# Attention by pairs of heads on half-array products, and a retention result laid out by features

## The chip, the cores and the metric

The kernel runs on one core of a Trainium2 chip. The metric is the device time of one execution in microseconds (us), as a median of several runs; lower is better. A core has a matrix engine (PE; the loading of its stationary operand is listed apart as PEld), a vector engine (DVE), a scalar engine (ACT), a general engine (POOL) and a queue that issues most of the transfers (SP). Each engine takes its instructions strictly in the order of its queue.

## The reference, cut to what matters

Two layers on 512 tokens of 1024 features. In each layer a modulated RMSNorm is projected to a wide vector, four mixers of 256 features each work on parts of it, one output projection and a SwiGLU follow. The change touches two mixers:

```python
def fox_attention(q, k, v, f_logit, f_bias):          # 4 heads of 64
    log_f = jax.nn.log_sigmoid((f_logit + f_bias).astype(jnp.float32))
    cum = jnp.cumsum(log_f, axis=1).transpose(0, 2, 1)
...
        s = jnp.einsum('bqhd,bkhd->bhqk', qb, k).astype(jnp.float32) * scale
        s = s + cq[..., :, None] - cum[:, :, None, :]
...
        p = jax.nn.softmax(s, axis=-1).astype(v.dtype)
        return jnp.einsum('bhqk,bkhd->bqhd', p, v)

def retention(q, k, v, g, positions, gn_g):            # 4 heads of 64, chunks of 128
...
    intra = jnp.einsum('bnhqk,bnkhe->bnqhe', intra_s, vc)
    kv = jnp.einsum('bnkhd,hk,bnkhe->bnhde', kc, zeta, vc)
...
        cross = jnp.einsum('bqhd,bhde->bqhe', q_n, state)
...
    o = (intra + cross).reshape(B, S, H, Dh).astype(jnp.float32)
    mu = jnp.mean(o, axis=-1, keepdims=True)
    var = jnp.mean(jnp.square(o - mu), axis=-1, keepdims=True)
    o = (o - mu) * lax.rsqrt(var + EPS) * gn_g.reshape(H, Dh).astype(jnp.float32)
    return jax.nn.silu(g) * o
```

## The kernel before, in words

Activations lie with features on the 128 partitions and the 512 tokens along the free axis. Every large projection is made of three products on split operands (`mm3`, lines 260 to 262), whose weights arrive by DMA in `raw` (L154, L152), are rounded on ACT (`wh`, L159) and corrected on DVE (`wl`, L164). Products of plain f32 operands, which the mixers use, appear in the trace as two passes each.

A layer runs the projections one after the other in the order of a written list (`MO` for layer 0, `MO1` for layer 1). The mixers are Python generators: `slot()`, called after each projection, advances every running generator by its rate from the table `KN`, so that their instructions are emitted between the projections. `finish_bg` runs a generator to its end where its result is needed. A scheduler then settles the order of each engine's queue. The output projection takes eight mixed pieces `mix[0..7]`: 0 and 1 from attention, 2 and 3 from pooling, 4 and 5 from retention, 6 and 7 from the convolution. Its first half (`do_o`) uses 2, 3, 6 and 7, the second half 0, 1, 4 and 5.

Attention (`fox_gen`) goes by single heads. `decay(h)` spreads the cumulated log forget gate of a head over all partitions with a product (L793), copies it (L795) and adds the causal mask (L797). `scores(h, i)` multiplies query block i with the keys up to it (L804; 64 rows of the array, since a head has 64 features), adds the decay while it takes the row minimum (L807, L811, L814), exponentiates on ACT (L816) and takes the reciprocal of the row sum (L817). `turn` transposes the unnormalized weights (L825) and copies them (L827), three steps later. `weigh` multiplies them with the values, four steps later (L838; 64 columns move), so that tokens come out on the partitions, and scales by the reciprocal (L841 on DVE in layer 0, L843 on ACT in layer 1). Once a pair of heads is done, four transposes (L847) bring features back to the partitions.

Retention (`ret_gen`) goes by pairs: transposed keys (L888), scores of both heads (L899), states (L913 to L921; here the two heads already write to the two column halves), results with tokens on the partitions (L931 on 128 rows, alternating with L933 on 64 rows), squares and their sums (L936, L938), normalization (L942), a transpose back (L949) and the product with the gate (L950). Rotary positions are applied on DVE (L875 to L879) from a copy that a DMA shuffles (L874).

The convolution (`conv_gen`) is 60 DVE instructions per layer (L735), then a normalization that goes PE, DVE, ACT, DVE, PE, DVE, POOL, PE (L741 to L753).

PSUM tiles come from two rings: three banks `mm` for projections, four banks `sm` for everything else.

Of the kernel before, what the change touches and what calls it, by code (L numbers as in the profile page):

```python
# [9 lines left out]
F32 = mybir.dt.float32  # L10
# [23 lines left out]
KN = {'GA': 3, 'GA1': 3, 'TR': 'V', 'NH': 5, 'NH1': 5, 'ST': ((0, 1), (1, 1), (2, 2), (4, 1), (5, 1), (6, 1), (7, 1)), 'bot': 1, 'MO': 'pu rk rq rg rv o o o o', 'MO1': 'pu rk rv rq o o o rg o', 'GK': 4, 'RD': 'sync', 'MM': 3, 'SM': 4, 'FB': 1, 'FB1': 2, 'FS': 'V', 'FS1': 'A', 'PT': 'A', 'PT1': 'A', 'LAGT': 3, 'LAGW': 4, 'OUTP': 0.0, 'FRONT': 1, 'FRONT1': 0, 'r_rot': 2, 'r_ada': 0.6, 'r_conv': 0.7, 'r_fox': 0.85, 'r_ret': 1, 'r_pool': 0.3, 'r_adaV': 0.4, 'q_conv': 1, 'q_fox': 1.2, 'q_ret': 2, 'q_pool': 0.4, 'q_adaV': 1, 'bP': 4, 'bPT': 2, 'bt': 3, 'brx': 2, 'bmx': 6, 'br8': 4, 'bpl': 3, 'brP': 3, 'bada': 3, 'bacs': 3, 'NR': 2, 'NW': 4, 'N1': 3, 'N11': 1, 'YLG': 9, 'SC': ('AVPPPGPA', 'GGPAVVPP', 'VVVVVVPP', 'VVVVVGVP', 'AAVPAVVP', 'VVVVVVVP', 'VVVVVVVP', 'AAVPAVVP'), 'SH': ('AVAPPPPP', 'VPPPPPAP', 'AAGAAAPP', 'AAAAAAPP', 'AAAAAAGP', 'AVVGAAVG', 'AAAAAAPP', 'AAAAAAPP'), 'MS': '', 'OF': {'lc': -1.907, 'lwq': -2.817, 'lw': -2.364, 'lh': -2.036, 'sc': -1.65, 'ds': 0.034, 'sh': -2.846, 'pc': -0.763, 'mc': -2.466, 'ph': -0.991, 'mh': 0.907, 't': 0.871, 'yh': -1.858, 'yl': 0.927, 'wh': -0.208, 'wl': -2.386, 'whq': -1.469, 'wlq': -0.219, 'mm': 0.333, 'mq': -0.566, 'dq': 0.84}, 'KB': (-4.084, -0.552, 1.672, 3.163, 4.202, 4.915, 6.134, 7.492), 'OA': (1, 0, 2, 3), 'OA1': (0, 1, 3, 2), 'OB': (1, 2, 0, 3), 'OB1': (1, 3, 0, 2), 'LAGW1': 4, 'LAGT1': 3, 'OUTP1': 3.0}  # L34
# [3 lines left out]
BUFS = dict(pw=2, ada=KN["bada"], ared=2, qk=4, acs=KN["bacs"], v=2, ff1=1, ff2=1, ff3=1, ff4=1, cumD=1, P=KN["bP"], rP=KN["brP"], PT=KN["bPT"], mx=KN["bmx"], ot=KN["bot"],  # L38
# [7 lines left out]
def trunk(ctx, tc, x, c, positions, ada_w, ada_b, norm_mix_g, norm_ffn_g, w_in, fox_fb,  # L46
# [8 lines left out]
    ps = ctx.enter_context(tc.tile_pool(name="ps", bufs=1, space=PSUM))  # L55

# [44 lines left out]
    sel = const([P, 32], "sel")  # L101
    eps = const([P, 1], "eps")
# [673 lines left out]
    def fox_gen(l, q, k, v):  # L776
# [10 lines left out]
        A.copy(cum[0:4, :], pt[0:4, :])  # L787
        yield
        head, prob, prT, outp, outt = {}, {}, {}, {}, {}

        def decay(h):
            pb = small()
            PE.matmul(pb, ident[0:4, h:h + 1].to_broadcast([4, P]), cum[0:4, :], start=True, stop=True)  # L793
            cb = held("ah1")
            A.copy(cb, pb)  # L795
            cd = tmp("cumD")
            V.tensor_tensor(out=tri(cd, P), in0=tri(cb, P), in1=tri(bigm, P).to_broadcast([P, 4, P]), op=ALU.add)  # L797
            head[h] = (cb, cd)

        def scores(h, i):  # L800
            cb, cd = head[h]
            pair, r0, w = h // 2, 64 * (h % 2), (i + 1) * P
            st = small()
            PE.matmul(st[:, 0:w], q[pair][r0:r0 + 64, i * P:w], k[pair][r0:r0 + 64, 0:w], start=True, stop=True)  # L804
            pr = tmp("P")
            mx = tmp("mx")
            V.tensor_tensor_reduce(out=pr[:, i * P:w], in0=st[:, i * P:w], in1=cd[:, i * P:w], scale=1.0,  # L807
                                   scalar=3e38, op0=ALU.add, op1=ALU.min, accum_out=mx[:, 0:1])
            m = mx[:, 0:1]
            if i > 0:  # L810
                V.tensor_tensor_reduce(out=pr[:, 0:i * P], in0=st[:, 0:i * P], in1=cb[:, 0:i * P], scale=1.0,  # L811
                                       scalar=3e38, op0=ALU.add, op1=ALU.min, accum_out=mx[:, 1:2])
                m = mx[:, 2:3]
                V.scalar_tensor_tensor(out=m, in0=mx[:, 0:1], scalar=mx[:, 1:2], in1=mx[:, 0:1],  # L814
                                       op0=ALU.min, op1=ALU.min)
            A.activation(pr[:, 0:w], pr[:, 0:w], AF.Exp, bias=m, scale=-1.0, accum_out=mx[:, 4:5])  # L816
            V.reciprocal(mx[:, 5:6], mx[:, 4:5])  # L817
            prob[h, i] = (pr, mx)

        def turn(h, i):  # L820
            pr, mx = prob.pop((h, i))
            w = (i + 1) * P
            tt = small()
            for j in range(i + 1):
                PE.transpose(tt[:, j * P:(j + 1) * P], pr[:, j * P:(j + 1) * P], ident)  # L825
            prT[h, i] = (tmp("PT"), mx)
            (A.copy if KL("PT", l) == "A" else V.tensor_copy)(prT[h, i][0][:, 0:w], tt[:, 0:w])  # L827

        def weigh(h, i):
            pair = h // 2  # L830
            pT, mx = prT.pop((h, i))
            if i == 0:
                outp[h] = small()
                if h % 2 == 0:
                    outt[pair] = tmp("ot")
            po = outp[h][:, i * 64:(i + 1) * 64]
            for j in range(i + 1):
                PE.matmul(po, pT[:, j * P:(j + 1) * P], v[:, j, h * 64:(h + 1) * 64], start=j == 0, stop=j == i)  # L838
            o = outt[pair][:, i * P + 64 * (h % 2):i * P + 64 * (h % 2) + 64]
            if KL("FS", l) == "V":  # L840
                V.tensor_scalar(out=o, in0=po, scalar1=mx[:, 5:6], scalar2=None, op0=ALU.mult)  # L841
            else:
                A.activation(o, po, AF.Copy, scale=mx[:, 5:6])  # L843
            if h % 2 == 1 and i == 3:
                pt = small()
                for t in range(4):
                    PE.transpose(pt[:, t * P:(t + 1) * P], outt[pair][:, t * P:(t + 1) * P], ident)  # L847
                mix[pair] = act_pair(pair)
                split(mix[pair], pt)

        todo = [(h, i) for h in range(4) for i in range(4)]
        decay(0)
        yield
        n = len(todo)
        for s_ in range(n + KL("LAGW", l)):
            if s_ < n:
                scores(*todo[s_])
            if 0 <= s_ - KL("LAGT", l) < n:
                turn(*todo[s_ - KL("LAGT", l)])
            if 0 <= s_ - KL("LAGW", l) < n:  # L860
                weigh(*todo[s_ - KL("LAGW", l)])
            if s_ < n and todo[s_][1] == 3 and s_ + 1 < n:
                decay(todo[s_][0] + 1)
            yield
# [16 lines left out]
    def ret_gen(l, pair, q, k, vbox, outs, sg):  # L881
# [433 lines left out]
```

## Time and profile before

| | |
|---|---|
| median of 3 runs (lowest, highest) | 1289.13 us (1285.33, 1296.54) |
| the profiled execution, its own time | 1290.33 us |
| its span, first to last instruction | 1288.5 us |
| mean granted PE clock | 0.964 |
| busy: PE, DVE, ACT, POOL | 1239.6, 758.0, 418.1, 100.8 us |
| attention's products on PE, layer 0 and layer 1 | 124 to 246 us, 755 to 825 us |
| retention's products on PE, layer 0 and layer 1 | 161 to 265 us, 818 to 864 us |
| convolution on DVE (L735), layer 0 and layer 1 | 80 to 186 us, 700 to 762 us |

The profile's page gives busy times, the groups of instructions and the waits. A busy time of PE counts overlapped and waiting matmuls in full, so the true step of a matmul is read from the chain of waits, which lists in order of time what ended last, with the count of instructions (x) in each piece.

### The profile page before, as it was taken

Reading aid. Unit: us, or ns where it says so; the run is one execution under the profiler, and the core shown is the slowest. Engines: PE = TensorE matmul, PEld = TensorE weight load, DVE = VectorE, ACT = ScalarE, POOL = GpSimd, SP = SyncE. Lnnn points to the kernel's source line nnn. Section 1 sums busy time; section 2 is a strip of 40 time slices with the busy share of each in tenths; the row PEclk is TensorE's granted clock in tenths of the full one; section 3 lists DMA queues with packets and bytes.
Section 4 is the critical chain, followed back from the end, with each engine's and each line's share of the span. In section 5 each row is a group of like instructions: output and inputs, shape, how many; then the busy total and the mean of one; then the engine's idle time right before and its main releaser. Section 6 shows DMA issues by size and latency. Waiting matters only on the chain.

```text
span 1288.5 us, 16684 instructions
## 1 busy us (share of the span) xinstructions
PE 1239.6 (96%) x6325; PEld 1029.5 (80%) x6325; DVE 758.0 (59%) x1324; ACT 418.1 (32%) x682; POOL 100.8 (8%) x183
## 2 busy tenths in 40 slices
PE   9999999999987999999999999889999999999997
PEld 8788677889875888888899877668988888888887
DVE  6789996467777655353357995355773333343333
ACT  5443333234221222222234244423432222222222
POOL 5542300101000000000000000000100000000000
PEclk8999977899998999999999999889999999999999
DMA  9766512124776736343233322012372333333321
GB/s 308 204 198 197 172 60 74 44 72 140 229 230 220 219 109 194 106 139 95 74 94 97 101 83 64 19 49 82 108 215 88 96 98 98 86 94 98 94 86 66
DMA packets 222552, 157.93 MB, mean 123 GB/s; under 512 B 8238, under 2 KB 197896, under 8 KB 222472
## 3 DMA queue, kind: packets, MB, share of 16 engines
q1 hardware_dynamic: 222312, 156.80, 40.7%
q8 instruction: 50, 0.82, 0.3%
q14 instruction: 30, 0.25, 0.1%
q10 hardware_dynamic: 160, 0.06, 0.0%
HBM read 152.64 MB, written 2.10 MB: 120 GB/s over the span
## 4 chain that ended last, share of the span: by engine, by line
PE 75%; DVE 5%; DMA 4%; issue 1%; ACT 1%; POOL 0%; DVEq 0%; SPq 0%; POOLq 0%; ACTq 0%
PE mm L260 22%; PE mm L261 21%; PE mm L262 21%; DMA ada<-in_ada_w 4%; PE sm L804 1%; DVE acs L315 1%; PE sm L838 1%; PE sm L931 1%; DVE wl L164 1%; PE sm L825 1%; PE sm L260 1%; PE sm L261 1%; PE sm L933 1%; PE sm L262 1%; PE sm L899 1%
## 5 line engine op out<-in xcount | busy, mean ns | idle before, releaser
L159 ACT CAST wh<-raw 128x1024 fp32r<-128x1024 f32 (+3 forms) x196 | 198.8, 1015 | 581.9 <-PE mm L261 354.9
L260 PE MATMUL mm<-yh,wh 128*128 128x512 f32 (+1 forms) x984 | 368.1, 381 | 7.3 <-ACT yh L433 6.5
L261 PE MATMUL mm<-yl,wh 128*128 128x512 f32 (+1 forms) x984 | 370.6, 378 | 2.8 <-DVE yl L437 2.8
L262 PE MATMUL mm<-yh,wl 128*128 128x512 f32 (+1 forms) x984 | 369.2, 377 | 0.0
L164 DVE TENSOR_TENSOR wl<-raw,wh 128x1024 fp32r<-128x1024 f32 (+3 forms) x196 | 231.5, 1181 | 137.1 <-ACT wh L159 131.5
L260 PEld LDWEIGHTS mm<-yh,wh 128*128 128x128 f32 x984 | 183.6, 189 | 43.5 <-ACT yh L433 7.6
L261 PEld LDWEIGHTS mm<-yl,wh 128*128 128x128 f32 x984 | 186.1, 189 | 39.2 <-DVE yl L437 3.8
L262 PEld LDWEIGHTS mm<-yh,wl 128*128 128x128 f32 x984 | 186.2, 189 | 36.1 <-issue 0.2
L260 PE MATMUL mm<-ah,wh 128*128 128x512 f32 (+1 forms) x516 | 191.3, 374 | 11.4 <-ACT ah L474 8.8
L261 PE MATMUL mm<-al,wh 128*128 128x512 f32 (+1 forms) x516 | 190.4, 369 | 0.4 <-DVE al L475 0.4
L262 PE MATMUL mm<-ah,wl 128*128 128x512 f32 (+1 forms) x516 | 189.9, 369 | 0.0
L315 DVE SCALAR_TENSOR_TENSOR acs<-ada,cact,acs 128x512 f32<-128x512 f32 x140 | 104.7, 748 | 47.0 <-DMA ada<-in_ada_w 44.9
L1039 DVE SCALAR_TENSOR_TENSOR xT<-mm,mod,xT 128x512 f32<-128x512 f32 (+1 forms) x86 | 57.6, 674 | 116.9 <-PE mm L262 116.8
L260 PEld LDWEIGHTS mm<-ah,wh 128*128 128x128 f32 x516 | 98.4, 191 | 28.5 <-ACT ah L474 9.2
L261 PEld LDWEIGHTS mm<-al,wh 128*128 128x128 f32 x516 | 98.1, 190 | 17.6 <-DVE al L475 1.0
L262 PEld LDWEIGHTS mm<-ah,wl 128*128 128x128 f32 x516 | 98.3, 190 | 17.2
L1219 DVE TENSOR_TENSOR t<-t,mm 128x512 f32<-128x512 f32 x42 | 28.8, 686 | 103.1 <-PE mm L262 103.1
L735 DVE SCALAR_TENSOR_TENSOR hc<-hp,cwT,hc 128x512 f32<-128x512 f32 x120 | 85.3, 743 | 1.0 <-ACT hc L732 0.9
L403 POOL TENSOR_TENSOR r<-r,mhalf 128x2 f32<-128x2 f32 (+3 forms) x16 | 17.3, 1079 | 580.4 <-DVE r L411 580.4
L654 POOL COPY ada<-yl 128x1 f32<-128x1 f32 x80 | 47.2, 596 | 139.8 <-DVE acs L315 95.2
L261 PE MATMUL mm<-wl,yh 128*128 128x256 f32 (+1 forms) x128 | 39.4, 308 | 0.0
L433 ACT ACTIVATE yh<-t,mod 128x256 fp32r<-128x256 f32 (+1 forms) x56 | 27.9, 533 | 35.1 <-DVE t L424 27.4
(257 smaller groups left out, 1256.4 us busy)
## 6 DMA issues: line engine op xcount, KB each, us to landing
raw<-in_ffn_w SPq DMA_DIRECT2D x104, 512.0 KB, 4.0
ada<-in_ada_w SPq DMA_DIRECT2D x160, 256.0 KB, 3.8
raw<-in_w_in SPq DMA_DIRECT2D x32, 512.0 KB, 4.5
raw<-in_ffn_w SPq DMA_DIRECT2D x32, 448.0 KB, 3.7
ad<-in_ada_w SPq DMA_DIRECT2D x32, 256.0 KB, 5.9
raw<-in_w_out SPq DMA_DIRECT2D x32, 256.0 KB, 3.0
raw<-in_w_in SPq DMA_DIRECT2D x4, 520.0 KB, 4.8
xn<-in_x SPq DMA_DIRECT2D x4, 512.0 KB, 6.5
```

The lines of the kernel that those rows point to most:

```text
L159: A.copy(h[:, 0:n], raw)
L164: V.tensor_tensor(out=lo[:, 0:n], in0=raw, in1=f(h[:, 0:n]), op=ALU.subtract)
L260: PE.matmul(o, lh, rh, start=start, stop=False)
L261: PE.matmul(o, lh, rl, start=False, stop=False)
L262: PE.matmul(o, ll, rh, start=False, stop=stop)
L315: V.scalar_tensor_tensor(out=acc, in0=r, scalar=ck, in1=acc, op0=ALU.mult, op1=ALU.add)
L403: G.tensor_tensor(out=out_, in0=ms, in1=mhalf[:, 0:ms.shape[-1]], op=ALU.pow)
L433: A.activation(yh[k][:, u:v], y, AF.Identity, bias=shift(l, i, k), scale=1.0)
L654: G.tensor_copy(t_[:, 0:1], f(yl[k][:, at:at + 1]))
L735: V.scalar_tensor_tensor(out=hcs[j], in0=hps[j][:, t:t + S], scalar=cwT[:, l, j, t:t + 1], in1=hcs[j], op0=ALU.mult, op1=ALU.add)
L1039: V.scalar_tensor_tensor(out=xT[:, n, u:v], in0=b[:, u:v], scalar=mod[l][:, gcol + n:gcol + n + 1], in1=xT[:, n, u:v], op0=ALU.mult, op1=A ...
L1219: V.tensor_tensor(out=t_, in0=t_, in1=b3, op=ALU.mult)
```

## The change

Attention works on two heads at once. The two heads' score products are issued side by side, on rows 0 to 63 and rows 64 to 127 of the array, into two banks. The weights are normalized on DVE before they are transposed. The product with the values has the values as the stationary operand, so its result comes out with features on the partitions: head 0 on column half 0 to 63, head 1 on 64 to 127 of one bank; the transposes at the end are gone. The cumulated gate goes out to DRAM with one transfer and comes back with four that spread it over the partitions. `turn` follows one step behind the scores and `weigh` two; a step is now a pair of heads.

Retention's scores are written alternately for the two row halves, its result is formed by features in one bank, the sums of squares are taken by a product with `hones`, and the reciprocal root is spread by a product and multiplied in at the end. `outs[pair]`, for which pair 1 waits, is now set after the gate of pair 0 is there.

```diff
-        def decay(h):
-            pb = small()
-            PE.matmul(pb, ident[0:4, h:h + 1].to_broadcast([4, P]), cum[0:4, :], start=True, stop=True)
-            cb = held("ah1")
-            A.copy(cb, pb)
+        cbs = [held("ah0"), held("al0"), held("ah1"), tmp("cb")]
+        cd = dr.tile([4, S], F32, tag="cum", name=nm("cumd"))
+        A.dma_start(cd, cum[0:4, :])
+        for h in range(4):
+            nc.sync.dma_start(cbs[h], cd[h:h + 1, :].to_broadcast([P, S]))
...
+        def scores(pair, i):
+
+            w = (i + 1) * P
+            sts = [small(), small()]
+            for hh in range(2):
+                r0 = 64 * hh
+                PE.matmul(sts[hh][:, 0:w], q[pair][r0:r0 + 64, i * P:w], k[pair][r0:r0 + 64, 0:w], start=True, stop=True)
+            for hh in range(2):
...
+                A.activation(pr[:, 0:w], pr[:, 0:w], AF.Exp, bias=m, scale=-1.0, accum_out=mx[:, 4:5])
+                V.reciprocal(mx[:, 5:6], mx[:, 4:5])
+                V.tensor_scalar(out=pr[:, 0:w], in0=pr[:, 0:w], scalar1=mx[:, 5:6], scalar2=None, op0=ALU.mult)
+                prob[h, i] = pr
...
+        def weigh(pair, i):
+
+            if i == 0:
+                outp[pair] = small()
+            pts = [prT.pop((2 * pair + hh, i)) for hh in range(2)]
             for j in range(i + 1):
...
+                for hh in range(2):
+                    h = 2 * pair + hh
+                    PE.matmul(outp[pair][64 * hh:64 * hh + 64, i * P:(i + 1) * P], v[:, j, h * 64:(h + 1) * 64],
+                              pts[hh][:, j * P:(j + 1) * P], start=j == 0, stop=j == i)
+            if i == 3:
                 mix[pair] = act_pair(pair)
-                split(mix[pair], pt)
...
+                split(mix[pair], outp[pair])
...
-        po = [small(), small()]
+
+        po = small()
         for n in range(4):
             for hh in range(2):
                 h = 2 * pair + hh
+                PE.matmul(po[64 * hh:64 * hh + 64, n * P:(n + 1) * P], v[:, n, h * 64:(h + 1) * 64],
+                          prs[hh][:, n * P:(n + 1) * P], start=n == 0, stop=False)
+        for n in range(1, 4):
+            for hh in range(2):
                 r0 = 64 * hh
...
+                PE.matmul(po[r0:r0 + 64, n * P:(n + 1) * P], st[n - 1][r0:r0 + 64, :],
+                          q[r0:r0 + 64, n * P:(n + 1) * P], start=False, stop=n == 3)
         sq = tmp("t")
...
+        A.activation(sq, po, AF.Square)
+        yield
+        pt = aux_cols(8)
+        for t in range(4):
+            PE.matmul(pt[:, 2 * t:2 * t + 2], sq[:, t * P:(t + 1) * P], hones, start=True, stop=True)
+        r = token_rsqrt(pt, 8, 1.0 / 64)
         yield
         while len(sg) <= pair:
             yield
...
+        o = outs[pair] = tmp("qk")
+        V.scalar_tensor_tensor(out=o, in0=po, scalar=hcol("gng", l * 2 + pair), in1=sg[pair], op0=ALU.mult, op1=ALU.mult)
+        pb = small()
+        for t in range(4):
+            for hh in range(2):
+                PE.matmul(pb[64 * hh:64 * hh + 64, t * P:(t + 1) * P],
+                          r[:, 2 * t + hh:2 * t + hh + 1].to_broadcast([P, 64]), ident, start=True, stop=True)
+        V.tensor_tensor(out=o, in0=o, in1=pb, op=ALU.mult)
```

The entries of `KN` that set the old lags and engines (`bot`, `FS`, `PT`, `LAGT`, `LAGW`) are gone; all other entries keep their values. The mask tile `cumD` has two buffers instead of one, and `ot` is gone.

On PE, towards the end of attention in layer 1, before; `sm` is a PSUM bank, `al` the queries and keys of heads 2 and 3, `P` the weights, `PT` their transposes, `v` the values:

```order
L804 MATMUL sm_6858<-al_1062_5965,al_1060_5963 128x384
L825 MATMUL sm_6867<-ident,P_6719 128x128 x4
L804 MATMUL sm_6893<-al_1062_5965,al_1060_5963 128x512
L838 MATMUL sm_6791<-v_6110,PT_6851 128x64 x3
L825 MATMUL sm_6902<-ident,P_6781 128x128
L825 MATMUL sm_6944<-ident,P_6840 128x128 x2
L838 MATMUL sm_6791<-v_6110,PT_6872 128x64 x4
```

and the same place now (L812 scores, L838 transposes, L850 the product with the values):

```order
L812 MATMUL sm_6767<-al_1049_5957,al_1047_5955 128x384
L850 MATMUL sm_6764<-PT_6733,v_6102 64x128
L812 MATMUL sm_6768<-al_1049_5957,al_1047_5955 128x384
L838 MATMUL sm_6830<-ident,P_6711 128x128 x2
L838 MATMUL sm_6835<-ident,P_6719 128x128 x2
L850 MATMUL sm_6764<-PT_6833,v_6102 64x128
L812 MATMUL sm_6846<-al_1049_5957,al_1047_5955 128x512
L812 MATMUL sm_6847<-al_1049_5957,al_1047_5955 128x512
L850 MATMUL sm_6764<-PT_6838,v_6102 64x128
```

The transposes now belong to the step just before the scores at their side, where before three heads' steps lay between; one of the two score pairs has a product of another kind between its halves.

On DVE in layer 1, before: retention pair 0's sums and normalization (L938, L942), attention's last split (L475), then the rotary of pair 1's queries (L875 to L879):

```order
L938 TENSOR_REDUCE r_1268_7041<-t_7038 128x8
L475 TENSOR_TENSOR al_7092<-sm_7086,ah_7091 128x512
L411 TENSOR_SCALAR r_1269_7043<-r_1268_7041 128x8
L942 TENSOR_TENSOR qk_7046<-sm_7022,r_1269_7043 128x4x64
L942 TENSOR_TENSOR qk_7046<-sm_7023,r_1269_7043 128x4x64
L875 TENSOR_TENSOR qk_7069<-rx_7067,cos_t 128x512
L877 TENSOR_TENSOR qk_7069<-qk_7069,rx_7070 128x512
L879 TENSOR_TENSOR qk_7069<-qk_7069,cs 128x512
```

and the last steps of the same rotary now (L884, L885, L887), with the scores and normalization of attention's steps (L818, L822, L828, L829) around it:

```order
L829 TENSOR_SCALAR P_6504<-P_6504,mx_6505 128x512
L828 RECIPROCAL mx_6603<-mx_6603 128x1
L884 TENSOR_TENSOR rx_7053<-rx_7053,sin_t 128x512
L829 TENSOR_SCALAR P_6602<-P_6602,mx_6603 128x128
L828 RECIPROCAL mx_6609<-mx_6609 128x1
L885 TENSOR_TENSOR qk_7052<-qk_7052,rx_7053 128x512
L829 TENSOR_SCALAR P_6608<-P_6608,mx_6609 128x128
L818 ISA P_6711,mx_6712<-sm_6707,cumD_6557 128x128
L818 ISA mx_6712 128x1
L822 ISA P_6711,mx_6712<-sm_6707,ah_1087_6254 128x128
L822 ISA mx_6712 128x1
L887 TENSOR_TENSOR qk_7052<-qk_7052,cs 128x512
```

The rotary has moved from behind retention pair 0's normalization to between attention's steps.

On SP in layer 0, the four transfers that bring the gate back stand here now, between the rotary's shuffle (L882) and the modulation weights (L354):

```order
L354 DMA ada_2224<-in_ada_w 128x512
L882 DMA rx_1376<-rx_1373 32x512 x4
L797 DMA ah_190_1106<-cumd_1110 128x512
L797 DMA al_191_1107<-cumd_1110 128x512
L797 DMA ah_192_1108<-cumd_1110 128x512
L797 DMA cb_1109<-cumd_1110 128x512
L354 DMA ada_2228<-in_ada_w 128x512
```

Nothing stood between those two before; the transfers behind them now follow the four.

More of the change, by code (lines that the diff above doesn't have):

```diff
@@ L796, in decay @@
             cd = tmp("cumD")
[L797 to L818, printed above, removed]
@@ L820, in turn @@
-        def turn(h, i):
-            pr, mx = prob.pop((h, i))
-            w = (i + 1) * P
-            tt = small()
-            for j in range(i + 1):
[L825 to L847, printed above, removed]
@@ new lines, in turn @@
+        def turn(pair, i):
+            w = (i + 1) * P
+            for h in (2 * pair, 2 * pair + 1):
+                pr = prob.pop((h, i))
+                tt = small()
+                for j in range(i + 1):
+                    PE.transpose(tt[:, j * P:(j + 1) * P], pr[:, j * P:(j + 1) * P], ident)
+                prT[h, i] = tmp("PT")
+                A.copy(prT[h, i][:, 0:w], tt[:, 0:w])
+        def weigh(pair, i):
+            if i == 0:
+                outp[pair] = small()
+            pts = [prT.pop((2 * pair + hh, i)) for hh in range(2)]
+            for j in range(i + 1):
+                for hh in range(2):
[3 more added lines that the diff above has]
+            if i == 3:
@@ L892, in ret_gen @@
                          AF.Identity, scale=ccol(4 + 2 * pair + hh))
+        sts = [small(), small()]
+        for n in range(4):
+            for hh in range(2):
+                r0 = 64 * hh
+                PE.matmul(sts[hh][:, n * P:(n + 1) * P], k[r0:r0 + 64, n * P:(n + 1) * P],
+                          q[r0:r0 + 64, n * P:(n + 1) * P], start=True, stop=True)
         prs = []
@@ L895, in ret_gen @@
             h = 2 * pair + hh
-            r0 = 64 * hh
-            st = small()
-            for n in range(4):
-                PE.matmul(st[:, n * P:(n + 1) * P], k[r0:r0 + 64, n * P:(n + 1) * P],
-                          q[r0:r0 + 64, n * P:(n + 1) * P], start=True, stop=True)
             pr = tmp("rP")
-            V.tensor_tensor(out=tri(pr, P), in0=tri(st, P),
+            V.tensor_tensor(out=tri(pr, P), in0=tri(sts[hh], P),
                             in1=tri(cs[:, C_DM + h * P:C_DM + (h + 1) * P], P).to_broadcast([P, 4, P]), op=ALU.mult)
             prs.append(pr)
-            yield
+        yield
         while not vbox:
@@ L946, in ret_gen @@
             yield
[L947 to L950 removed]
+        o = outs[pair] = tmp("qk")
+        V.scalar_tensor_tensor(out=o, in0=po, scalar=hcol("gng", l * 2 + pair), in1=sg[pair], op0=ALU.mult, op1=ALU.mult)
+        pb = small()
+        for t in range(4):
+            for hh in range(2):
+                PE.matmul(pb[64 * hh:64 * hh + 64, t * P:(t + 1) * P],
+                          r[:, 2 * t + hh:2 * t + hh + 1].to_broadcast([P, 64]), ident, start=True, stop=True)
+        V.tensor_tensor(out=o, in0=o, in1=pb, op=ALU.mult)
         mix[4 + pair] = act_pair(4 + pair)
```

62 lines of the change are left out of this document (34 added, 28 removed).

## The prediction

> **What bounds the kernel now.** I read the busy times first, then engine by engine the stretches that hold attention and retention, then the chain of waits inside those stretches, and last the single waits on PE.
>
> ```profile
> PE 1239.6 (96%) x6325; PEld 1029.5 (80%) x6325; DVE 758.0 (59%) x1324; ACT 418.1 (32%) x682; POOL 100.8 (8%) x183
> core 0: us, PE busy (x) PEld busy (x) DVE busy (x) ACT busy (x) POOL busy (x), PEclk, DMA share, GB/s
> 100.00:186.00 86.00, 82.98 (x389) 62.35 (x387) 84.91 (x188) 32.42 (x60) 22.17 (x35) 0.92 0.52 154
> 186.00:206.00 20.00, 19.82 (x107) 14.52 (x106) 12.37 (x47) 9.46 (x22) 0.00 (x0) 0.91 0.17 54
> 206.00:226.00 20.00, 17.81 (x76) 15.98 (x75) 12.48 (x22) 5.95 (x11) 2.34 (x6) 0.57 0.20 66
> 755.00:781.00 26.00, 26.00 (x153) 19.69 (x152) 20.79 (x62) 12.28 (x27) 0.45 (x4) 0.93 0.18 54
> 808.00:838.00 30.00, 24.24 (x166) 19.21 (x165) 11.61 (x38) 11.79 (x34) 1.64 (x1) 0.87 0.00 1
> 838.00:855.00 17.00, 12.90 (x69) 9.70 (x70) 7.69 (x15) 5.67 (x10) 1.01 (x1) 0.74 0.09 20
> ```
>
> PE is busy 96% of the span, so a product that goes away counts in full unless another engine is the bound where it stands. There is one such place. In layer 0, from 100 to 186 us, DVE works 84.91 of 86 us (the convolution, the modulation and attention at once); PE looks busy there too, but PE work saved there buys nothing. From 186 us in layer 0, and all through layer 1, DVE has gaps and PE sets the pace. The clock falls to 0.57 where the convolution's normalization and retention stand alone (206 to 226), so the same products take longer there. The end of the mixers in layer 1 is a chain:
>
> ```profile
> PE sm L899 <- DVE qk L879: 5.7, 1, 5.7
> 810.39 0.41 PE sm L804 x2
> 814.48 1.05 PE sm L804 x2
> 823.37 1.03 PE sm L931 x8
> 824.41 0.89 PE sm L838 x8
> 825.30 0.37 PE sm L933 x4
> ...
> 827.72 0.36 PE sm L933 x2
> 828.08 0.60 PE sm L847 x4
> 828.70 0.59 ACT ah L474
> ...
> 830.17 1.65 POOL r L403
> ...
> 834.79 3.06 PE sm L899 x16
> 837.85 3.09 PE sm L741 x4
> ...
> 853.88 0.90 PE mm L260 x3
> ```
>
> PE waits 5.7 us there for the rotary of pair 1's queries (L879), which stands on DVE behind a normalization that waits for POOL (L403, 1.65). Then come L899, the convolution's normalization from 837.85 to about 849, and the output projection from 853.88.
>
> **What PE loses, per layer at full clock.** A plain f32 product is two passes, so the x2 of L804 is one product. Spreading the gate (L793) is a product 512 wide like the last L804: four of them, 4 x 1.05 = 4.2 us. L847 goes, 2 x 0.60 = 1.2. L949 is four transposes of the same kind, at the step of the L825 row below, 0.12 each: 2 x 4 x 0.12 = 1.0.
>
> Scores of one head take from 0.41 (128 wide) to 1.05 (512 wide), mean 0.73, so 4 x 4 x 0.73 = 11.7. If two row halves run side by side, half goes: 5.9; if not, nothing.
>
> L838 has 80 passes per layer at 0.89/8 = 0.11, 8.8 us. The new form moves 128 columns instead of 64. Whether that costs, and whether two heads overlap, is read here:
>
> ```profile
> 203.65 0.12 PE sm L825
> 203.76 0.50 PE sm L913 x12
> 204.26 1.93 PE sm L741 x4
> ```
>
> A product that moves 128 columns steps by 0.12, no more than the 64 of L838, so the step is not set by the columns. L913, whose two heads already write to the two column halves, makes 12 passes in 0.50, 0.042 each: less than half a step. Column halves do run side by side. So 40 pairs at 0.11 are 4.4, and 4.4 are saved; without overlap 0.
>
> Retention's result: from 823.37 to 828.08, less the 0.89 of L838, are 3.8 us for one pair of heads (28 passes, 0.13 to 0.18 each). The new one is 14 paired passes at 0.11 plus 0.3 for going between full rows and halves (L933, in alternation, takes 0.36 for two passes, 0.14 over 2 x 0.11, and there are two changes): 1.8. Two pairs save 4.0; without overlap 28 x 0.11 = 3.1, which saves 1.4.
>
> Added are the sums of squares (L951, 8 passes, 0.9 a pair) and the spread (L961, 16 passes in two column halves, 0.9 + 0.3 a pair): 4.2; without overlap (L961 16 x 0.11) 6.0. Together per layer: -4.2 - 1.2 - 1.0 - 5.9 - 4.4 - 4.0 + 4.2 = **-16.5**; if no half overlaps, -4.2 - 1.2 - 1.0 - 1.4 + 6.0 = -1.8.
>
> Against one term stands a rule. L944 writes two row halves to one bank, which no run here shows; its three pairs of products per pair of heads are counted as overlapping. The Trainium skill, TensorEngine Tiling (Array Packing), Restrictions and Gotchas, says that different row tiles cannot use the same PSUM bank at the same time. By it L944 would gain nothing, and the sum would be 4 x 6 x 0.11 = 2.6 us higher; no trace here bears on it.
>
> **DVE.** The weights are normalized in 32 instructions, 128 to 512 wide.
>
> ```profile
> L313 DVE TENSOR_SCALAR acs<-ada,cact 128x512 f32<-128x512 f32 x20 | 9.5, 476 | 5.5 <-DMA ada<-in_ada_w 5.4
> L841 DVE TENSOR_SCALAR ot<-sm,mx 128x64 f32<-128x64 f32 x16 | 4.5, 279 | 6.0 <-PE sm L838 4.6 <-PE sm L847 1.4
> L938 DVE TENSOR_REDUCE r<-t 128x8 f32<-128x512 f32 x4 | 2.7, 683 | 6.4 <-ACT t L936 6.3
> L942 DVE TENSOR_TENSOR qk<-sm,r 128x256 f32<-128x256 f32 x8 | 3.0, 416 | 1.9 <-POOL r L403 1.8
> L797 DVE TENSOR_TENSOR cumD<-ah,cs 128x512 f32<-128x512 f32 x8 | 5.5, 684 | 5.5 <-ACT ah L795 5.5
> L807 DVE CUSTOM_DVE_ANT_0 P<-sm,cumD 128x128 f32<-128x128 f32 x32 | 8.8, 285 | 9.1 <-PE sm L804 9.1
> L811 DVE CUSTOM_DVE_ANT_0 P<-sm,ah 128x384 f32<-128x384 f32 x8 | 4.4, 552 | 0.0
> ```
>
> The same operation took 0.279 (64 wide) and 0.476 (512 wide): 32 of them are 8.9 to 15.2, about 12. L841, L938 and L942 go (4.5 + 2.7 + 3.0), and four full-width products with the spread come (L963, 4 x 0.684 = 2.7). DVE gains +1.4 to +7.7 over both layers. Only in the saturated stretch does that cost time: 10 of 16 head steps lie there, where a normalization (some 0.35) replaces an L841 (0.279), so about +1 (0 to 3).
>
> **The bounce through DRAM.** No write to DRAM of this kind is in the trace.
>
> ```profile
> rx<-rx SPq DMA_DIRECT2D x32, 64.0 KB, 2.5
> 126.28 0.58 ACT L787 COPY al<-sm 4x512 f32<-4x512 f32 x1 [2.86 <-PE sm L784]
> 137.01 0.69 DVE L797 TENSOR_TENSOR cumD<-ah,cs 128x512 f32<-128x512 f32 x1
> 757.85 0.58 ACT L787 COPY al<-sm 4x512 f32<-4x512 f32 x1 [5.30 <-PE sm L784]
> 765.66 0.28 DVE L807 CUSTOM_DVE_ANT_0 P<-sm,cumD 128x128 f32<-128x128 f32 x1
> ```
>
> The nearest row is the rotary's shuffle, 2.5 us; out and back is about 5, plus up to 2.5 behind such a shuffle on SP. The gate is ready at 126.9 and 758.4, so the copies land at 132 to 134.5 and 763.5 to 766. First use was at 137.0 in layer 0 (covered), and at 765.7 in layer 1, behind one mask addition of 0.69: between 1.5 early and 1 late. I take 0, bound +3: while DVE waits for a copy (L803), the convolution, the weights' corrections and the splits queue behind it. On SP the modulation weights and the output weights follow the four transfers; DVE, which needs them, is behind with its own work there, so a delay of one such hop is taken as free, with 2.5 as its bound.
>
> **The wait that goes, and the new ones.** The rotary no longer stands behind the normalization, so the 5.7 us in layer 1 go. What is late next is PE's own work and the convolution's normalization, which starts earlier by the same amount. A new wait can come from the short lag: transposes follow one step behind the scores. For the longest step, DVE takes 2 x (0.285 + 0.552) = 1.7 for two heads, the exponential about 0.6 (as L474, 0.59), the normalization 0.48: 2.8 with almost nothing for handing over. In between PE has the previous transposes (8 x 0.12, less for shorter steps) and the next scores, 1.05: about 2.0 (the product with the values stands there too, but waits for a copy itself). So 0.8 us is missing in each step without projections beside it: five steps in layer 1 (4.0), three in layer 0 (2.4). Bounds are 0 (projections fill in) and 2 a step.
>
> **The sum.** Layer 1: -16.5 - 5.7 + 4.0 = -18.2. Layer 0, only what lies after 186 us: 6 of 16 head steps of scores, L838 and L847, (5.9 + 4.4 + 1.2) x 6/16 = -4.3; one gate spread, -1.0; L949, -1.0; retention's second pair, -2.0; its first, at the low clock:
>
> ```profile
> 215.59 0.85 PE sm L931 x4
> ...
> 219.53 1.37 PE aux L371 x6
> ...
> 224.32 0.62 PE sm L933 x2
> ```
>
> These are 9.35 us less the 1.37 of L371, so 8.0; the new 14 passes at 0.85/4 and 0.3 come to 3.3: -4.7. Added +4.2, DVE +1, new waits +2.4: **-5.4**. Both layers: -23.6. The profiled execution took 1290.3, 1.2 above the median, so 1266.7 there and **1265** as a median.
>
> **Rivals.** *The halves do not run side by side.* L913 speaks against it for columns; for row halves in two banks nothing speaks either way. With only the row halves failing, scores save nothing: 2 x 5.9 less what lies under DVE, +8, 1273. With all failing, layer 1 gives -1.8 - 5.7 + 4.0 = -3.5, and layer 0 has 6.0 + 1 + 2.4 added against 0.4 + 1.0 + 1.0 + 0.7 and 28 passes at 0.21 in place of 8.0 (2.1), +4.2: 1290.
>
> *The tail is paced by DVE and ACT.* Each of the eight tail steps lacks 2 us more than counted, because a second head's exponential and normalization queue behind the first's: +16, 1281. For it: DVE has 2 x (0.285 + 0.552 + 0.476) = 2.6 us per longest step, before its small instructions, against PE's 1.05 + 8 x 0.12 + 8 x 0.11 = 2.9, so neither has room. Against it: DVE was only 11.61 of 30 us busy from 808 to 838. The Trainium skill says in TensorEngine Tiling (Array Packing), Performance Considerations, that packing speeds TensorE up but not the reading of PSUM, which can become the bottleneck; L807 and L811 are that reading, and their times are unchanged per head.
>
> *Slower.* The same wait, at PE's queue, in all 16 steps: products of the projections stand behind a transpose in strict order, so where DVE is late (it has 84.91 of 86 us to do already in layer 0, 20.79 of 26 in layer 1) they wait too. At 2.8 us a step, one whole chain, this is 45 less the 6.4 counted: 1304. It decides from 2.7 a step on (1302). The clock of 0.57 after waits speaks for more loss, PE's 26.00 of 26 with the present lags against it.
>
> **Chances.** Forecast 0.64, with the row halves' failure in it, 1253 to 1276 (0.05 of it below 1250); tail paced by DVE 0.15; no overlap 0.08; slower 0.13. The range 1250 to 1290 leaves out the 0.05, the last case and a little of the third, and holds the bounds of the bounce and of the waits. One per cent is 12.9 us (1276.2 and 1302.0), about what a measurement of this kernel can tell from no change: faster 0.63, same 0.25, slower 0.12.
>
> **What would show it.** In the changed profile two L812 of 512 should take about 1.05 together, and L850 about 0.11 for two passes of two heads; 2.1 and 0.22 would mean no overlap. The pair L939 and L944 should take 1.8; 2.4 would mean that the shared bank counts. The wait for L887 should be gone; waits of PE at L838 for the normalization (L829) show the new price, 0.8 a step by me, over 2.7 by the last rival. L803 should not wait over 3 us for a transfer. The prediction is wrong if DVE's time from 100 to 186 grows by more than 3, or if layer 1's output projection starts less than 10 us earlier, counted from the start of its attention.

## The result, and the profile after

The changed kernel took 1256.79 us as a median (1255.27 to 1258.75), against 1287.56 for the kernel before in the same session; the ratio is 0.9749, with a 95% interval of 0.970 to 0.9799. The forecast was 1265 with a range of 1250 to 1290. The gain is 2.5% where 1.9% was forecast (1265 from 1289.13). The profiled execution took 1255.27 us by its own time, its span is 1253.5.

Busy times and stretches of the changed kernel (columns as in the prediction; the stretches end earlier because the work does):

```profile
PE 1209.0 (96%) x6373; PEld 1004.1 (80%) x6373; DVE 761.2 (61%) x1332; ACT 406.5 (32%) x654; POOL 95.5 (8%) x186
100.00:186.00 86.00, 78.06 (x387) 60.08 (x386) 84.64 (x183) 29.45 (x56) 17.52 (x35) 0.93 0.56 165
186.00:206.00 20.00, 18.37 (x118) 12.39 (x116) 15.94 (x57) 10.43 (x25) 0.00 (x0) 0.97 0.16 54
206.00:220.00 14.00, 12.23 (x88) 10.50 (x89) 9.77 (x18) 5.84 (x10) 2.79 (x8) 0.76 0.30 94
783.00:801.00 18.00, 15.62 (x132) 10.51 (x130) 9.66 (x36) 8.30 (x20) 0.16 (x1) 1.00 0.01 2
801.00:818.00 17.00, 14.86 (x102) 12.09 (x102) 7.74 (x16) 5.46 (x9) 2.87 (x2) 0.80 0.12 31
```

From 100 to 186 us DVE is as full as before (84.64 of 86) and PE's saving only makes PE idle (78.06 where it was 82.98). The gain begins behind that. DVE's total rose by 3.2 us.

To see where time went, I take three moments that every kernel here has, from the trace: the start of the 17th addition of an output projection's result to the stream (L1039, now L1052: 98 of them in each kernel), the start of layer 1's convolution, and the 69th such addition. Before, they stand at 280.4, 699.6 and 906.1 us, the last addition at 1280.1. Differences to the kernel before, in us, each from the one profiled execution of a kernel:

| kernel | mixing, layer 0 | up to layer 1's convolution | mixing, layer 1 | rest | all |
|---|---|---|---|---|---|
| changed | -14.8 | -4.1 | -18.7 | +1.5 | -36.1 |
| changed, once more | -14.2 | -2.1 | -18.7 | +1.5 | -33.4 |
| attention alone | -5.2 | -1.8 | -9.9 | +1.6 | -15.3 |
| the same, retention's result in two groups | -12.8 | +0.1 | -7.3 | +2.8 | -17.3 |
| retention alone | -12.5 | -1.1 | -8.8 | +1.5 | -20.9 |
| no transfer through DRAM | -10.9 | +0.3 | -14.5 | +5.4 | -19.7 |
| scores on the same rows | -14.1 | -5.0 | -16.2 | +1.5 | -33.8 |
| product with the values by head | -15.0 | +2.2 | -17.2 | +4.9 | -25.1 |
| retention's products by head | -12.2 | -1.5 | -15.4 | +1.5 | -27.6 |
| scores ahead of that product | -18.5 | -0.3 | -16.3 | +4.6 | -30.5 |
| normalization twice | -11.9 | -0.2 | -13.0 | +1.5 | -23.6 |
| no normalization | -17.4 | -0.8 | -19.5 | +5.4 | -32.4 |
| every second one on ACT, layer 1 | -15.2 | -1.8 | -18.5 | +1.5 | -34.0 |

The forecast had -5.4 for layer 0's mixing, -18.2 for layer 1's and nothing elsewhere. In the two profiled executions of the changed kernel the mixing stages repeat within 0.6 us. The stage in between doesn't: it holds a wait of PE for layer 0's feed-forward input, which hangs on the stream of modulation weights. In the kernel before, and now:

```profile
PE mm L260 <- ACT ah L474: 8.8, 1, 8.8
```

```profile
PE mm L265 <- ACT ah L479: 6.2, 2, 5.8
PE sm L838 <- DVE P L829: 2.6, 4, 1.2
PE sm L905 <- ACT rP L899: 0.9, 1, 0.9
```

It was 6.9 when the same kernel ran again. The last column follows the granted clock: behind layer 1's mixing the clock stands at 0.50 for 3.4 us in the kernels with +1.5 or +1.6, for 6.8 or 10.2 us in those with +2.8 to +5.4, and not at all in the kernel before. What a kernel gains or loses outside the two mixing stages is therefore not put down to its edit directly. The last two rows show that the wait for the rotary is gone (L905 waits for nothing but 0.9 of ACT), and that the new wait of PE for normalized weights is 2.6 us: 2.4 in layer 0, all before 186 us, and 0.3 in layer 1.

The chain of waits of the changed kernel, at the end of attention and retention in layer 0 (first four rows) and layer 1:

```profile
194.15 0.84 PE sm L812 x2
194.99 0.36 PE sm L850 x2
195.36 0.84 PE sm L812 x2
198.55 1.11 PE sm L812 x4
...
784.86 1.06 PE sm L812 x4
788.72 0.87 PE sm L850 x10
791.32 1.08 PE sm L905 x8
792.40 0.36 PE sm L850 x2
795.16 0.93 PE sm L939 x15
796.09 1.91 PE sm L746 x4
798.01 0.83 PE sm L944 x12
799.51 1.07 PE aux L951 x8
806.60 1.91 PE sm L961 x16
812.21 0.96 PE mm L265 x3
```

Two score products of 512 take 1.06 to 1.11 where one took 1.05. But at 194.15 a piece of L850 stands between the two heads' products, and each takes its full 0.84. L850 costs 0.87 for ten passes in one piece, and 0.36 for the two passes of one head alone.

### The profile page after: what moved, and what is told of

It is laid out like the page before. It is cut to its first block, busy times and chain, and to the rows that moved or that the text cites. A ratio compares the mean times of both kernels' runs of the same rounds, so it can differ in the third digit from the quotient of the medians.

```text
span 1253.5 us, 16762 instructions
## 1 busy us (share of the span) xinstructions
PE 1209.0 (96%) x6373; PEld 1004.1 (80%) x6373; DVE 761.2 (61%) x1332; ACT 406.5 (32%) x654; POOL 95.5 (8%) x186
## 4 chain that ended last, share of the span: by engine, by line
PE 74%; DMA 5%; DVE 4%; issue 1%; ACT 1%; POOL 0%; DVEq 0%; ACTq 0%
PE mm L265 22%; PE mm L266 22%; PE mm L267 22%; DMA ada<-in_ada_w 4%; DVE acs L320 1%; PE sm L812 1%; PE sm L850 1%; PE sm L265 1%; PE sm L266 1%; PE sm L267 1%; DVE wl L169 1%; DMA raw<-in_ffn_w 1%; PE sm L838 1%; PE aux L404 0%; PE sm L961 0%
## 5 line engine op out<-in xcount | busy, mean ns | idle before, releaser
L265 PE MATMUL mm<-yh,wh 128*128 128x512 f32 (+1 forms) x984 | 369.5, 382 | 5.2 <-ACT yh L438 5.2
L265 PEld LDWEIGHTS mm<-yh,wh 128*128 128x128 f32 x984 | 185.4, 191 | 40.6 <-ACT yh L438 6.2
L265 PE MATMUL mm<-ah,wh 128*128 128x512 f32 (+1 forms) x516 | 189.4, 370 | 6.2 <-ACT ah L479 6.2
L266 PE MATMUL mm<-al,wh 128*128 128x512 f32 (+1 forms) x516 | 189.8, 368 | 0.8 <-DVE al L480 0.8
L1052 DVE SCALAR_TENSOR_TENSOR xT<-mm,mod,xT 128x512 f32<-128x512 f32 (+1 forms) x86 | 57.7, 675 | 117.1 <-PE mm L267 116.8
L265 PEld LDWEIGHTS mm<-ah,wh 128*128 128x128 f32 x516 | 97.3, 189 | 24.0 <-ACT ah L479 6.8
L267 PEld LDWEIGHTS mm<-ah,wl 128*128 128x128 f32 x516 | 97.6, 189 | 17.1 <-issue 0.2
L659 POOL COPY ada<-yl 128x1 f32<-128x1 f32 x80 | 42.0, 531 | 153.7 <-DVE acs L320 103.1
L265 PE MATMUL mm<-wh,yh 128*128 128x256 f32 (+1 forms) x128 | 39.4, 308 | 2.7 <-DVE v L1124 2.7
```

Of the source, the lines that this page charges most:

```text
L265: PE.matmul(o, lh, rh, start=start, stop=False)
L266: PE.matmul(o, lh, rl, start=False, stop=False)
L267: PE.matmul(o, ll, rh, start=False, stop=stop)
L659: G.tensor_copy(t_[:, 0:1], f(yl[k][:, at:at + 1]))
L1052: V.scalar_tensor_tensor(out=xT[:, n, u:v], in0=b[:, u:v], scalar=mod[l][:, gcol + n:gcol + n + 1], in1=xT[:, n, u:v], op0=ALU.mult, op1=A ...
```

## The experiments

**Each half alone.** The kernel before with the new retention, and the changed kernel with the old retention. Of the second edit, cut to a few lines:

```diff
-        po = small()
+        po = [small(), small()]
...
-        A.activation(sq, po, AF.Square)
...
-        pt = aux_cols(8)
...
+        pt = small()
+        for n in range(4):
+            PE.transpose(pt[:, n * P:(n + 1) * P], o[:, n * P:(n + 1) * P], ident)
```

> The change to attention alone, retention as before. If the gain is the sum of the products that each part saves: attention saves 10 to 12 us in layer 1 and about 4 in layer 0 after 186 us, so 15 of the 32 us, about 1272. If retention's new form gives nothing of its own (its added products eat what it saves), nearly all of it: 1257 to 1261.

> The change to retention alone, attention as before. If the gain is the sum of the products saved: 7 us in layer 0 (retention's result ran there at the low clock), and in layer 1 the wait of 5.7 us for the rotary of pair 1's queries goes only if the rotary moves forward without the attention's change; 8 to 14 us faster than before, about 1276. If retention's added products eat its gain: within 4 us of before.

The ratios here and below are to the kernel before, in the same session. Attention alone: 0.9906 (0.9871 to 0.9941). Retention alone: 0.9837 (0.981 to 0.9864). The two gains of 0.94% and 1.63% add up to about the 2.51% of the whole. By stages they do so in layer 1 (9.9 and 8.8 against 18.7); in layer 0 5.2 and 12.5 are more than the 14.8 of both, so there they overlap. The half with many more added products brings more. Retention gives 12.5 us in layer 0, where I had expected 7. With attention alone the wait for the rotary stays:

```profile
PE sm L907 <- DVE qk L887: 6.3, 1, 6.3
```

With retention alone no wait of that kind is left, though attention there is the old one. So it is retention's new order that frees the rotary: pair 1's queries no longer stand behind a normalization that waits for POOL.

**The granted clock.** What else retention brings in layer 0 is in the stretches from 206 us on. First the kernel before, then attention alone, retention alone, the changed kernel, a fence for each:

```profile
206.00:216.00 10.00, 7.81 (x40) 7.58 (x39) 5.17 (x11) 1.72 (x4) 1.57 (x4) 0.64 0.09 27
216.00:226.00 10.00, 10.00 (x38) 8.40 (x38) 7.32 (x12) 4.23 (x8) 0.77 (x2) 0.50 0.32 104
```

```profile
216.00:226.00 10.00, 10.00 (x36) 8.50 (x36) 6.57 (x12) 4.04 (x9) 1.79 (x3) 0.50 0.22 71
```

```profile
216.00:226.00 10.00, 9.88 (x73) 8.35 (x71) 8.47 (x16) 3.60 (x6) 2.48 (x3) 0.98 0.16 51
```

```profile
216.00:226.00 10.00, 9.23 (x75) 6.96 (x76) 8.13 (x14) 4.77 (x10) 2.15 (x2) 1.00 0.17 50
```

All kernels drop to 0.50 after the convolution's normalization has let PE wait. With the old retention the clock stays there until about 229 us, with the new one until 214 to 216, and PE then runs twice as many instructions in the same time (73 and 75 against 38 and 36). Is it the going back and forth between full rows and row halves that holds it down? Against attention alone, with indices cut to [...]:

```diff
-                PE.matmul(o_, prs[hh][...], v[...], start=True, stop=n == 0)
-                if n > 0:
-                    PE.matmul(o_, q[...], st[n - 1][...], start=False, stop=True)
+                PE.matmul(o_, prs[hh][...], v[...], start=n == 0, stop=False)
+        for n in range(1, 4):
+            for hh in range(2):
+                PE.matmul(po[hh][...], q[...], st[n - 1][...], start=False, stop=n == 3)
```

> Attention changed, retention as before except that its result is formed in two groups: first all products on full rows, then all on row halves, in place of going back and forth. If going back and forth is what kept the granted clock at 0.50 from 216 to 229 us in layer 0: it returns to 1.00 soon after 216, and 28 passes take 3 to 4 us there instead of 8; 6 to 9 us faster than attention's change alone, 1267 to 1269. If it is the layout with tokens on the partitions (64 columns moving): the clock stays at 0.50 and the gain is that of fewer changes, 1 to 2 us.

```profile
206.00:216.00 10.00, 8.33 (x53) 7.93 (x54) 6.17 (x11) 3.14 (x5) 1.94 (x6) 0.73 0.30 89
216.00:226.00 10.00, 10.00 (x35) 7.77 (x35) 6.21 (x13) 2.51 (x6) 1.64 (x1) 0.59 0.12 42
```

Layer 0's mixing became 7.6 us shorter than with attention alone, as the first case said, but the clock did not come back at 216: it did at about 224. The whole kernel came out at 0.9848 (0.9809 to 0.9888), hardly faster than attention alone, since layer 1's mixing grew by 2.6: there the clock stood at 0.50 for 23.9 us in this profile, against 17.1 with attention alone. So neither case holds as written. The slow stretch behind 206 us is 20.5 us in both profiles with the old retention, 13.7 with fewer changes, and 3.4 or 6.8 in all eleven profiles with the new form. Which part of the new form does it, 128 moving columns or fewer passes, no run separates.

Layer 1 has such a stretch too, at the end of its mixing. The kernel before, then the changed one:

```profile
830.00:840.00 10.00, 5.21 (x19) 3.97 (x20) 4.21 (x9) 0.04 (x1) 1.64 (x1) 0.50 0.01 2
840.00:850.00 10.00, 5.90 (x31) 4.54 (x30) 3.12 (x6) 1.48 (x3) 1.01 (x1) 0.67 0.00 0
```

```profile
800.00:810.00 10.00, 7.80 (x50) 6.89 (x49) 2.78 (x6) 3.13 (x6) 3.02 (x2) 0.66 0.00 0
810.00:820.00 10.00, 9.62 (x73) 7.13 (x72) 7.21 (x13) 3.42 (x6) 0.00 (x0) 1.00 0.21 54
```

In the records of the clock, layer 1's mixing has 20.5 us at 0.50 before (3.4 of them at 772) and 6.8 now. The changed kernel's own stretch in layer 0 was 6.8 us in one execution and 3.4 in the other, and 3.4 us at half the clock are about 1.7 us of PE's time: differences of a stage below that say little about an edit.

**No transfer through DRAM.** The gate is spread by products again.

```diff
-        cd = dr.tile([4, S], F32, tag="cum", name=nm("cumd"))
-        A.dma_start(cd, cum[0:4, :])
-        for h in range(4):
-            nc.sync.dma_start(cbs[h], cd[h:h + 1, :].to_broadcast([P, S]))
...
+            PE.matmul(pb, ident[0:4, h:h + 1].to_broadcast([4, P]), cum[0:4, :], start=True, stop=True)
+            A.copy(cbs[h], pb)
```

> The gate is spread by four products and copies again, no transfer through DRAM. By the prediction's sum: 4.2 us slower in layer 1 and 1 us in layer 0, +5, less up to 3 because twelve instead of eight score pairs stand side by side in this order: +2 to +5. If the transfers made DVE wait by as much as they saved PE: 0 or faster.

0.9856 (0.9825 to 0.9886), 14 us slower than the changed kernel. In the mixing stages the loss is 3.9 and 4.2 us. In layer 1 that is the price of four products of 1.05. In layer 0 all four stand before 186 us, where PE's work was to cost nothing; but DVE is busy there for 82.05 of the 86 us, where it had 84.64, and the convolution ends 2.6 us later (189.8 against 187.2). The other half of the loss lies outside the mixing stages; all four executions have it (1266.3 to 1271.9), and apart from the longer slow stretch behind layer 1 it is not explained. The transfers themselves hid almost entirely. In layer 1 of the changed kernel, the copy of the gate on ACT, then the first two mask additions on DVE:

```profile
738.97 0.57 ACT L792 COPY al<-sm 4x512 f32<-4x512 f32 x1 [5.30 <-PE sm L789]
```

```profile
744.16 0.69 DVE L803 TENSOR_TENSOR cumD<-ah,cs 128x512 f32<-128x512 f32 x1
745.44 0.69 DVE L803 TENSOR_TENSOR cumD<-al,cs 128x512 f32<-128x512 f32 x1 [0.59 <-DMA al<-cumd]
```

From the end of the copy to the second head's gate are 5.9 us, and DVE waits 0.59.

**Do the halves overlap?** Scores of both heads on the same rows; head by head in the product with the values; head by head in retention.

```diff
-                r0 = 64 * hh
+                r0 = 0
                 PE.matmul(sts[hh][:, 0:w], q[pair][r0:r0 + 64, ...
```

> Both heads' score products read rows 0 to 63 (head 1's scores are formed from head 0's queries and keys, so this part of the result is another one); the order of every engine is the same. If the row halves overlap and PE sets the pace: the eight pairs that still stand side by side on PE take twice their time. Of those, 256 and 512 wide in layer 0 after 186 us (0.63 + 1.05 = 1.7) and 128, 384, 512 and 512 wide in layer 1 (0.41 + 0.84 + 1.05 + 1.05 = 3.35) count: about 5 us slower than the changed kernel. If the chain of DVE and ACT sets the pace instead, the second product falls into PE's waits: under 1 us.

```diff
-            for j in range(i + 1):
-                for hh in range(2):
-                    h = 2 * pair + hh
+            for hh in range(2):
+                h = 2 * pair + hh
+                for j in range(i + 1):
```

> In attention's product with the values all products of head 0 come before those of head 1, so the column halves have nothing to overlap; the same products. If the overlap is what saves there: 40 passes of 0.11 us more in layer 1 and 27 of 40 in layer 0 after 186 us, 4.4 + 3.0 = 7 us slower than the changed kernel. If PE's waits for weights take it up: 2 or less.

> Retention's result and the spread of its root go head by head (L939, L944, L961), the same products without overlap. 8 + 6 + 8 passes of 0.11 more for each pair of heads: 2.4, over four pairs 9.7 us slower. If the granted clock after 216 us in layer 0 depends on how long these products take, it stays near 0.5 for longer and some 4 us are added: 14. If the shared bank of L944 or something else already kept them apart: under 5.

The ratios are 0.9781 (0.9754 to 0.9808), 0.9767 (0.9709 to 0.9824) and 0.9746 (0.9687 to 0.9804). The intervals are too wide for effects of this size, so the stages decide. Scores on the same rows:

```profile
784.18 0.84 PE sm L812 x2
786.33 1.91 PE sm L812 x4
```

The two products of 512 now take 1.91 where they took 1.06: row halves in two banks do run side by side. Layer 1's mixing lost 2.5 of the 3.35 us expected, layer 0's 0.7 of 1.7.

The product with the values lost 1.5 in layer 1 and nothing in layer 0, against 7 expected. From the start of each product to the start of the next, waits taken off, L850 takes 7.84 us in layer 1 in the changed kernel and 10.25 head by head; the old L838 took 9.43. The overlap is there, but the 40 pairs never cost 4.4. In layer 0 the slow stretch behind 206 us was 3.4 us in this profile, against 6.8, which can hide a loss. As a whole the four executions took 1261.5 to 1265.8 us, 7 more than the changed kernel as a median, as expected; but in the profiled one almost all of it stands outside the mixing stages, so that agreement is luck.

Retention head by head lost 2.6 and 3.3 us in the mixing stages, 6 against 9.7, and the clock came back at 216 us all the same. In that kernel the passes of L939, L944 and L961 in layer 1 took 9.4 us together against 6.8. But the edit takes only part of the overlap away: in its trace the second head's passes start beside the first head's, after its first two to four (L939 at 800.465 and 800.471). That is one reason for 6 instead of 9.7, and it leaves open what the clock would do with no overlap at all; with less of it the slow stretch in layer 0 stayed at 6.8 us. In layer 1 it was 10.2 against 6.8, which is part of the 3.3.

**Order of a step.**

```diff
-            if s_ >= 2:
-                weigh(*todo[s_ - 2])
             if s_ < n:
                 scores(*todo[s_])
+            if s_ >= 2:
+                weigh(*todo[s_ - 2])
```

> In each of attention's steps the scores are emitted ahead of the product with the values, not behind it. Eleven instead of eight pairs of scores stand side by side on PE, and the product with the values comes in 21 pieces instead of 28. If products cut apart are what was lost: 3 x 0.73 + 7 x 0.14 = 3 us faster than the changed kernel. If waits for the weights or for free banks take it up: no change, within 1.

0.9744 (0.9676 to 0.9812): no difference to the changed kernel that could be told. Layer 0's mixing, where seven of eight pairs stay together instead of four, gained 3.7 us; layer 1's lost 2.3. There this order keeps no more pairs together than before (four of eight; the scores take 9.31 us on PE instead of 8.20). The clock has a part in both: at 0.50 for 3.4 us less behind 206 us, and for 3.4 us more in layer 1.

**Is DVE the bound?** The normalization twice; not at all; and for every second head on ACT in layer 1.

```diff
                 V.tensor_scalar(out=pr[:, 0:w], in0=pr[:, 0:w], scalar1=mx[:, 5:6], scalar2=None, op0=ALU.mult)
+                V.tensor_scalar(out=pr[:, 0:w], in0=pr[:, 0:w], scalar1=1.0, scalar2=None, op0=ALU.mult)
```

> The normalized weights are multiplied by 1.0 once more on DVE: 32 instructions of 0.28 to 0.48 us more, 6 us of DVE work per layer. If DVE is the bound only from 100 to 186 us in layer 0: 10 of 16 head steps lie there, about 3.5 us, and little elsewhere, 4 us slower. If DVE and ACT pace attention's steps everywhere: twice 0.4 us a step in 16 steps, 11 to 13 us slower.

> The weights are not divided by their row sums (that multiplication on DVE is left out, so attention's part of the result is another one). By the prediction: its own +1 on DVE in layer 0 goes and the new waits of 0.8 us in eight steps shrink by the 0.48 of this link: 5 us faster than the changed kernel, 3 of it in layer 1. If DVE paces all of attention in layer 1: 6 us there, 8 to 10 in all. If neither is on the path: within 1.

> In layer 1 the weights of every second head are divided on ACT instead of DVE; the same computation. If DVE's amount of work paces attention in layer 1: 3 us of it move away, 2 to 3 us faster than the changed kernel. If the chain of one step paces it (scores, DVE, ACT, DVE, transposes): ACT is slower per instruction than DVE, no gain or up to 2 us slower.

Twice: 0.9803 (0.9746 to 0.9861), +2.9 us in layer 0's mixing and +5.6 in layer 1's. PE's waits for normalized weights, and for the copies of their transposes, are now

```profile
PE sm L839 <- DVE P L830: 10.1, 4, 5.2
PE sm L851 <- ACT PT L841: 3.2, 4, 1.0
```

where they were 2.6 and 1.8. But the 10.1 stand in layer 0 alone, 9.3 of them before 186 us. In layer 1 PE does not wait for normalized weights at all: the loss there is 3.8 us of other waits of PE (8.3 in all against 4.5; 1.7 more for the copies, 1.6 more for a projection's input, L265) and 1.8 us of longer products. Not at all: 0.972 (0.9686 to 0.9754), -2.6 and -0.8 us; the order on DVE is another one there, since the convolution in layer 0 ended at 194.4 us, not 187.2. On ACT: 0.9738 (0.9707 to 0.9769), no change in either stage. So 6 us more on DVE cost layer 1 nearly all of it, and 6 us less give back 0.8. The step's chain is just covered by PE's work: neither "DVE paces all of it" nor "only layer 0 is bound" is right. Whether DVE's amount of work or the length of the chain would be the limit is not shown: moving half of the normalization to ACT changed nothing, but leaving all of it out gave only 0.8.

**The changed kernel once more.**

> The changed kernel once more, to see which stages repeat. If the stages are fixed by the order: mixing of layer 0 and of layer 1 within 1 us of the first time, and PE's wait of 5.8 us in layer 0's feed-forward stage again. If that stage depends on when the modulation's transfers happen to run: a wait of 7 to 9 there, and 3 to 6 us more in the span, with the mixing as it was.

0.9743 (0.9705 to 0.978). Mixing was as before, with a wait of 6.9 instead of 5.8 behind it.

## Why the prediction was right, and where it was not

The sign, the place and the order of size were right: the gain lies behind 186 us in layer 0 and in layer 1's mixing. Layer 1 came out at -18.7 against -18.2. But its terms were not those of the sum, and the agreement is luck. PE's time by line in layer 1, in us, from starts to starts with waits taken off:

| term | before | after | difference | forecast |
|---|---|---|---|---|
| spreading the gate | 4.20 | 0 | -4.2 | -4.2 |
| L847, L949 | 2.01 | 0 | -2.0 | -2.2 |
| scores | 11.55 | 8.20 | -3.4 | -5.9 |
| product with the values | 9.43 | 7.84 | -1.6 | -4.4 |
| retention's scores | 5.17 | 4.40 | -0.8 | 0 |
| retention's result | 7.25 | 3.82 | -3.4 | -4.0 |
| L951, L961 | 0 | 4.71 | +4.7 | +4.2 |
| transposes of the weights | 4.77 | 5.33 | +0.6 | 0 |
| L741, now L746 | 3.15 | 1.92 | -1.2 | 0 |
| products of the projections | 139.2 | 137.0 | -2.1 | 0 |
| waits | 9.86 | 4.52 | -5.3 | -1.7 |

The terms of the sum for products, and the transposes, came out 7.2 us short. Against that stand 4.1 us of products for which the sum has nothing (retention's scores, L741, the projections), part of which ran at 0.50 before and at full clock now, and 3.6 us more saved in waits.

**Halves run side by side:** right, and each rival of no overlap falls. What was mis-sized is how often they stand side by side. I took every pair as a pair, although the order that I showed has a piece of another product between two score products. Four of eight score pairs in layer 1 are cut apart and save nothing, and the product with the values comes in part in pieces of one head that cost 0.36, for which the sum has 0.11. The reading that the step is not set by the columns holds for the full array only: on column halves a pair of passes that move 64 columns steps by 0.058 us (L922), one that moves 128 by 0.109 (L850). The 0.11 of the sum fits L850 all the same, and that is luck.

**New waits:** 0.8 us in each of eight steps was too much. In layer 1 PE waits 0.3 us for normalized weights and 0.9 for the copies of their transposes, where 4.0 was forecast, and in layer 0 not at all for weights behind 186 us, where 2.4 was. The transposes had more cover than the 2.0 us that I counted. Not in the sum at all is that the wait of the convolution's normalization (L399, now L404) fell from 2.8 to 0.9 us in layer 1. The rival of a tail paced by DVE and ACT was close, as the doubled normalization shows, but the undoubled one stayed under the cover; the slower rival needed 2.7 a step and had 0.3, the waits for copies included.

**The wait for the rotary:** right, and right for the reason given (5.7 before, 6.3 with attention alone, none with the new retention).

**The bounce:** right. 5.9 us of transfer against 5 to 7.5 estimated, 0.59 waited against 0 to 3.

**Layer 0:** too small by 9 us. The step that failed is "its first, at the low clock", -4.7, with nothing for what comes behind it. I priced retention's own products at the low clock and left the clock for the rest as it was. PE's time for them fell from 13.16 to 4.89 us for both pairs, 8.3 where -6.7 stood in the sum. The projections behind 186 us, which before ran at 0.50 until 229 and once more from 250 to 257, took 44.9 us for 230 products against 50.2 for 238: 195 ns on average against 211, which is 3.7 us. Retention's scores and the products that move one column (L371, L399) took 2.5 less. PE's waits grew by 1.0, where 2.4 stood in the sum. In the other direction, scores, L838 and L847 gave 2.4 of the 4.3 forecast.

**DVE in the saturated stretch:** +0.7 us at the end of layer 0's convolution (185.8 to 186.5), and +2.0 when the kernel ran again; +1 expected, 0 to 3 as bounds.

**L944 in one bank:** the two heads' passes start 6 ns apart in the changed kernel's trace and a pair takes 0.11. At clock 0.50 a pair steps by 0.21, as in L943 of the grouped kernel, where each head has a bank of its own. The rule that different row tiles cannot use one bank at the same time (the Trainium skill, TensorEngine Tiling (Array Packing), Restrictions and Gotchas) did not show here, where each head writes its own half of the partitions; 12 passes took 0.83 us with the change of mode, and 1.09 head by head, where part of them still overlap.

The 2 to 4 us gained between the mixing stages were not forecast. They go with PE's wait for the feed-forward input (8.8 us before, 5.8 and 6.9 now); why it is shorter is not shown.

## What to carry to other kernels

Products on half of the array are worth counting in the order in which they are issued: a pair that is cut apart by one other product saves nothing, and the cut costs a change of mode twice (0.36 us for two passes that step by 0.11). When many terms are summed, a total that agrees does not vouch for its terms; a table by line from the trace does. Where the clock is low after a wait, the cost of a form of product includes everything that runs until the clock is back.

## What the runs showed of the hardware

The granted clock was 1.00 or 0.50 in every record of the 14 profiles, and each stretch at 0.50 inside a trace lasted a whole multiple of 3.41 us. The one behind 206 us in layer 0 lasted 3.4 us (the changed kernel once more), 6.8 (the changed kernel and retention alone), 13.7 (retention's result in groups) and 20.5 (before, attention alone). The Trainium skill, TensorE: Matmul & The Clock Gate, Part 1, describes a clock at half rate or full, decided by activity in windows of about 3.4 us; the lengths agree. But it has the clock come back after one busy window, and here PE issued without a gap from 216 to 226 us at 0.50 in the kernel before. Most of what was running there moved 64 columns a pass and changed between full rows and row halves, with six passes of one column (L371) between. With 128 columns a pass the clock came back in layer 0 within two steps of 3.41 us.

What counts as activity stays open. The share of time in which the array streams columns does not decide it by itself: in the grouped kernel six products of 512 columns began between 217.4 and 220.8 us, behind passes of one column, and the next step was still at 0.50; head by head, 17 passes of 128 columns between 212.4 and 215.8 brought the clock back. No run tested this by itself.
